# Two more empty steps between the scaling of the context's rows and their transposes

## The chip, the cores and the metric

The kernel runs on one core of a Trainium2 chip. The metric is the time on the device in microseconds (us) of one execution, the median of several runs. The core has TensorE (PE in the profile; PEld is its loading of stationary operands), VectorE (DVE), ScalarE (ACT), GpSimd (POOL) and SyncE (SP), which here only issues DMAs. Each engine works through its own instruction queue; semaphores make one wait for another.

## The reference, cut to what matters

One layer of a diffusion backbone over 2048 latent tokens of width 1024, with a prefix of 256 context tokens. The change touches the part in which the context's keys and values are made:

```python
mod_c = jax.nn.silu(c_ctx) @ w_mod[l] + b_mod[l]
sh1c, sc1c, ... = jnp.split(mod_c, N_MOD, axis=-1)
h_c = modulate(ctx_s, norm1_g[l], sh1c, sc1c)      # rmsnorm(ctx) * g * (1 + scale) + shift
p_c = h_c @ w_in[l][:, :KV_COLS]                   # 256 x 1024 times 1024 x 256
k_c = rmsnorm(kv_heads(p_c[..., :K_W]), k_norm_g[l])
v_c = kv_heads(p_c[..., K_W:KV_COLS])
h_x = modulate(x, norm1_g[l], sh1, sc1)
p_x = h_x @ w_in[l]                                # 2048 x 1024 times 1024 x 3840
...
```

The latent tokens' projection `p_x` yields keys, values, queries, the two inputs of the spatial gating, and two gate logits. Attention over all latent and context keys, the gating, a merge, an output projection and an MLP follow.

## The kernel before

**Precision and products.** Every float32 product is done with operands split into a high and a low part, by a cast on ScalarE (or VectorE) and a subtraction on VectorE, and as three products on TensorE (`product`, lines 1744, 1745 and 1746: high by high, high by low, low by high). Large products use seven block products in place of eight, in the order `SUMS = (0, 1, 5, 6, 4, 2, 3)`; the sums of weight blocks that this needs are called terms. They are made on VectorE, written to `t_d` in memory, and loaded again (line 710) when their block product is due. The line 712 casts such a load and line 713 forms its low part.

**The projection** (`project`) runs over two blocks of 1024 tokens. In each, `pairs_run` goes through two pairs of weight column blocks: first pair 0 (keys, values, queries; 384 columns a block), then pair 1 (gating inputs; 512 columns). A pair is 14 steps: seven block products, two halves of the inner dimension each. A step is four token tiles of six products. In the first token block the run is split: pair 0, then the gates of two weight groups (`gates`, groups 0 and 1), then pair 1, then the other six groups.

**Work beside it.** Three kinds of side work are threaded into these steps as Python generators:

- `opening` (line 1136) is continued at two points of each pair step, by `next(opens, None)` in `along` (line 1197). In pair 0 that makes 28 visits, in pair 1 more; during the gates it is not continued. It first finishes the second token block's operands; then it lets visits pass until `CONTEXT_AT = 20` and hands over to `context_keys` (line 1176).
- `self.work` is a list of generators, of which `tick` (line 762) continues the first by one piece: twice a pair step, once a gate step. It holds the keys' work (`keys_work`, line 799: norm, rotation, split, transposes, store), the queries' work (`queries_work`, line 837), the weight terms of pair 1 (`terms`, line 664), the preparation of the spatial weights (`gm_consts`) and so on, in the order in which they were put in. The weight terms are put in at place 1 when pair 0 is done.
- the gate weights' preparation, advanced by the gate steps.

**`context_keys`** (line 963) loads the context's two row tiles (line 966), waits one visit, computes the root mean square and scales the rows (`h_scale`: squares on ScalarE, line 515; the reciprocal root on VectorE, lines 163 to 179, in which several other sums also run; the scaling on ScalarE, line 528), waits one visit, takes a bank for the accumulator `acc`, and then goes in four visits over the inner dimension, two rows of 128 at a time: a load of 256 KB of weights (line 976) and its split (lines 153 to 157), four transposes (line 999), the modulation on ScalarE (line 1003), a split, and the 12 products of the visit before. The products of the fourth part come at the visit after it, with the copies of keys and values out of `acc` (lines 1011 and 1014), the store of the values (line 1015), and this line, which puts the rest of the context's work behind what the list holds by then:

```python
        self.work += [self.keys_work(nt, None, kraw), self.gm_consts()]
```

**Tiles.** On-chip memory is divided into rings of slots by tag. Those that matter are "m" (four slots of 4 KB a partition) and "t2" (six), and the banks of TensorE's accumulators, four "a" for the pairs' tiles and four "b" for everything else (transposes, context, and the gate groups 0 and 1). In the profile the tags show as m, t, a and b. The context's row tiles, its split operands w and h, the squares, the queries' tiles and the weight terms' tiles are all of tag "m".

**Order.** The program's order of emission is the priority of an instruction. A scheduler fills each engine's queue at build time, taking the first by priority of those that its own model holds ready, so work of a lower priority can be put ahead of work that isn't ready. `order` (line 2069) adds that tiles of one tag are handed out in emission order; pinned stretches keep the engines' order as written, but the work of the change lies in none of them.

Of the kernel before, what the change touches and what calls it, by code (L numbers as in the profile page):

```python
# [72 lines left out]
class Kern:  # L73
# [889 lines left out]
    def context_keys(self):  # L963
        nc = self.nc
        nt = CTX // P
        xs = self.x_load(self.I["ctx"][0], nt, self.m4)
        yield
        self.h_scale(xs)
        yield
        acc = self.bank([nt, CTX])  # L970
        staged = None
        for k0 in range(0, KC + 2, 2):
            done, staged = staged, None
            if k0 < KC:
                raw = self.t2([2, 256])
                nc.sync.dma_start(
                    raw,
                    self.I["w_in"][0][k0 * P : (k0 + 2) * P, :256].rearrange(
                        "(k p) c -> p k c", p=P
                    ),  # L980
                )
            if done:
                w, h = done
                for j in range(2):
                    for t in range(nt):
                        tok = slice(t * P, (t + 1) * P)
                        a = (h[:, 0, j, tok], h[:, 1, j, tok])
                        self.product(
                            acc[:, t], [a], [(w[:, 0, j], w[:, 1, j])],
                            k0 == 2 and j == 0 and t == 0,  # L990
                        )
            if k0 < KC:
                w, h = (self.m4([2, 2, CTX], F32R) for _ in range(2))
                self.split(raw, w[:, 0], w[:, 1], lo_eng="dve")
                ps = self.bank([2, CTX])
                tmp = self.t2([2, CTX])
                for j in range(2):
                    for t in range(nt):
                        nc.tensor.transpose(
                            ps[:, j, t * P : (t + 1) * P], self.columns(xs[t], k0 + j),  # L1000
                            self.ident,
                        )
                    nc.scalar.activation(
                        tmp[:, j], ps[:, j], AF.Identity,
                        scale=self.G1[:, k0 + j, 1:2], bias=self.S1[:, k0 + j, 1:2],
                    )
                self.split(tmp, h[:, 0], h[:, 1], hi_eng="dve", lo_eng="dve")
                staged = (w, h)
                yield
        kraw, V = self.t2([TT, NKV, HD]), self.t2([TT, NKV * HD])  # L1010
        nc.vector.tensor_copy(
            kraw[:, :nt].rearrange("p t h d -> p t (h d)"), acc[:, :, :P]
        )
        nc.scalar.copy(V[:, :nt, :], acc[:, :, P:])
        nc.scalar.dma_start(self.vc_d[:, :nt], V[:, :nt])
        self.work += [self.keys_work(nt, None, kraw), self.gm_consts()]
        yield
# [1417 lines left out]
```

## Time and profile before

| | us |
|---|---|
| median of 3 runs | 3008.2 (3007.79 to 3643.23) |
| profiled execution, its own time | 3012.09 |
| its span | 3010.1 |
| mean granted TensorE clock | 0.993 |

The profile is of one execution. A row of its time-ordered view has the start and the duration in us, the engine, the line of the kernel, the operation, output and inputs by tag, and the shape; in brackets stand the idle time of that engine just before and what ended it. The chain of waits lists what ended last at each moment, with start and duration. A row of the table by stretches has the busy time and the instruction count of each engine, the granted TensorE clock (1.00 is full), the DMA engines' busy share and GB/s. Matmuls overlap, so their durations add up to more than the time they take.

The page's slices of 1/40 of the span (75.25 us each), busy tenths of TensorE and VectorE:

```profile
PE   7899999999999999999999989999999999999999
...
DVE  5857487766888887867555587776676766654555
```

The projection's first token block fills the first slices; the context's rows are loaded at 88.52 us, and the transposes of line 999 run from 110.75 to 126.8 us:

```profile
88.52 1.53 SPq L505 DMA_DIRECT2D m<-in_ctx  x2
...
104.37 0.46 SPq L976 DMA_DIRECT2D t<-in_w_in  x1
...
124.78 0.42 SPq L976 DMA_DIRECT2D t<-in_w_in  x1
```

The four weight loads of line 976 are issued by SyncE between 104.37 and 124.78 us.

### The profile page before, as it was taken

The page shows a single profiled execution, that of the slowest core. Times are in us where ns is not written, and L with a number is a line of the kernel's source. Part 1 is how long each engine was busy: PE and PEld are TensorE (multiplying, and loading weights), DVE is VectorE, ACT ScalarE, POOL GpSimd, SP SyncE. Part 2 cuts the span into 40 slices and gives each one's busy share as a digit, 9 for nine tenths or more (in the row PEclk, how much of TensorE's full clock was granted, in tenths as well). Part 3 has the DMA queues.
Part 4 walks back from the last instruction along what each step waited for, and adds up shares of the span by engine and source line. Part 5 has one row for each costly group of instructions (what it writes and reads, how often), then busy time and mean ns, then how long its engine had stood idle before and what let it go on. Part 6 is the DMA issues. An engine that isn't in the chain of part 4 may idle for free.

```text
span 3010.1 us, 37936 instructions
## 1 busy us (share of the span) xinstructions
PE 2931.4 (97%) x13325; PEld 2210.1 (73%) x13325; DVE 2069.9 (69%) x2983; ACT 1418.8 (47%) x2318; POOL 650.8 (22%) x470
## 2 busy tenths in 40 slices
PE   7899999999999999999999989999999999999999
PEld 5778788876455555556888878888887888888887
DVE  5857487766888887867555587776676766654555
ACT  5544865554454544444222354444454344444432
POOL 0000000001899898894212200000000000000000
PEclk9999999999999999999999999999999999999999
DMA  7687967774010010016776658888766544447554
GB/s 274 186 293 262 315 205 225 253 245 150 24 36 29 22 37 22 22 35 189 238 215 194 183 198 308 310 301 304 263 216 223 185 154 154 154 158 272 210 208 156
DMA packets 386175, 559.04 MB, mean 186 GB/s; under 512 B 38640, under 2 KB 192416, under 8 KB 385984
## 3 DMA queue, kind: packets, MB, share of 16 engines
q1 hardware_dynamic: 373616, 535.89, 53.7%
q10 hardware_dynamic: 12368, 20.73, 1.9%
q8 instruction: 105, 1.72, 0.2%
q14 instruction: 86, 0.70, 0.1%
HBM read 379.75 MB, written 176.69 MB: 185 GB/s over the span
## 4 chain that ended last, share of the span: by engine, by line
PE 82%; DMA 6%; DVE 6%; ACT 3%; issue 2%; SPq 1%; ACTq 0%; POOL 0%; DVEq 0%; POOLq 0%
PE b L1744 14%; PE b L1745 14%; PE b L1746 14%; PE b L2322 8%; PE b L2291 4%; PE b L2310 4%; PE b L186 4%; PE b L187 4%; PE b L188 4%; PE b L2246 3%; PE a L1744 2%; PE a L1746 2%; PE a L1745 2%; PE b L192 1%; DMA m<-ws_d 1%
## 5 line engine op out<-in xcount | busy, mean ns | idle before, releaser
L2257 DVE TENSOR_REDUCE ts<-b 128x1 f32<-128x512 f32 x492 | 302.0, 681 | 69.7 <-PE b L2246 69.7
L2342 POOL TENSOR_TENSOR ac<-ac,p 128x512 f32<-128x512 f32 x214 | 306.1, 1463 | 54.5 <-ACT p L2314 54.5
L1860 DVE TENSOR_TENSOR b<-b,b 128x1024 fp32r<-128x1024 f32 x170 | 200.7, 1221 | 137.1 <-ACT b L1859 136.3
L1859 ACT CAST b<-b 128x1024 fp32r<-128x1024 f32 x170 | 170.6, 1051 | 225.3 <-PE b L1746 100.1
L2314 ACT ACTIVATE p<-b 128x512 f32<-128x512 f32 x384 | 194.0, 624 | 175.5 <-PE b L2310 168.3
L1745 PE MATMUL b<-b,b 128*128 128x512 f32 x680 | 265.2, 390 | 3.6 <-DVE b L1860 3.5
L1744 PE MATMUL b<-b,b 128*128 128x512 f32 x680 | 266.2, 391 | 1.7 <-DVE f L1881 1.5
L1746 PE MATMUL b<-b,b 128*128 128x512 f32 x680 | 264.7, 389 | 0.0
L2342 POOL TENSOR_TENSOR ac<-p,p 128x512 f32<-128x512 f32 x32 | 51.5, 1629 | 746.1 <-DMA raw<-in_w_mod 736.8
L2342 POOL TENSOR_TENSOR ac<-ac,t 128x512 f32<-128x512 f32 x152 | 204.1, 1374 | 0.0
L2291 PE MATMUL b<-h,h 128*128 128x512 f32 x576 | 187.3, 405 | 3.3 <-ACT p L2314 2.2
L2322 PE MATMUL b<-p,h 128*64 128x512 f32 x768 | 187.3, 611 | 0.0
L2310 PE MATMUL b<-h,h 128*128 128x512 f32 x576 | 178.6, 391 | 0.0
L1745 PE MATMUL b<-hb,b 128*128 128x512 f32 x446 | 173.8, 390 | 0.0
L1754 DVE TENSOR_TENSOR f<-f,b 128x512 f32<-128x512 f32 x160 | 109.2, 682 | 78.4 <-issue 45.7
L1744 PE MATMUL b<-hb,b 128*128 128x512 f32 x415 | 161.9, 390 | 0.0
L1746 PE MATMUL b<-hb,b 128*128 128x512 f32 x415 | 161.3, 389 | 0.0
L1745 PEld LDWEIGHTS b<-b,b 128*128 128x128 f32 x680 | 127.6, 188 | 32.2 <-DVE b L1860 5.5
L2291 PEld LDWEIGHTS b<-h,h 128*128 128x128 f32 x576 | 103.6, 188 | 63.8 <-DVE ts L2257 24.3
L1744 PEld LDWEIGHTS b<-b,b 128*128 128x128 f32 x680 | 127.6, 188 | 29.9 <-ACT b L1859 2.8
L1746 PEld LDWEIGHTS b<-b,b 128*128 128x128 f32 x680 | 127.7, 188 | 26.5
L157 POOL TENSOR_TENSOR bw<-bw,bw 128x512 fp32r<-128x512 f32 x58 | 75.9, 1331 | 235.6 <-ACT bw L153 233.8
(440 smaller groups left out, 7243.0 us busy)
## 6 DMA issues: line engine op xcount, KB each, us to landing
ao_d<-f SPq DMA_DIRECT2D x224, 256.0 KB
f<-in_w_ff SPq DMA_DIRECT2D x48, 1024.0 KB
b<-ao_d SPq DMA_DIRECT2D x85, 512.0 KB
b<-w2o_d SPq DMA_DIRECT2D x85, 512.0 KB
w2o_d<-f SPq DMA_DIRECT2D x112, 256.0 KB
f<-in_w_in SPq DMA_DIRECT2D x38, 512.0 KB
f<-x_d SPq DMA_DIRECT2D x64, 256.0 KB
hb<-ao_d SPq DMA_DIRECT2D x54, 256.0 KB
```

The source lines that it names most:

```text
L186: mm(ps, sh, mh, start=start, stop=False)
L1744: mm(ps, wh, hh, start=start and k == 0, stop=False, skip_group_check=True)
L1745: mm(ps, wh, hl, start=False, stop=False, skip_group_check=True)
L1746: mm(ps, wl, hh, start=False, stop=k == len(w) - 1, skip_group_check=True)
L1859: nc.scalar.copy(h, f32(l))
L1860: nc.vector.tensor_tensor(out=l, in0=f32(l), in1=f32(h), op=ALU.subtract)
L2257: nc.vector.tensor_reduce(out=self.mx[:, t, h, c : c + 1], in_=ps[h], axis=AX.X, op=ALU.max)
L2291: self.nc.tensor.matmul(self.pts[j][h], k.KA[c][self.kv][:, ks], self.qa[h], start=True, stop=False, skip_group_check=True,)
L2310: self.nc.tensor.matmul(s, k.KB[c][self.kv][:, ks], self.qb[h], start=False, stop=True, skip_group_check=True,)
L2314: self.nc.scalar.activation(pt[h], s, AF.Exp)
L2322: nc.tensor.matmul(self.o[h * HD : (h + 1) * HD, :], k.V[c][:, i, self.kv * HD : (self.kv + 1) * HD], pt[h], start=j == 0, stop=j == NKT - 1,)
L2342: nc.gpsimd.tensor_tensor(out=self.acc[e][:, h], in0=old[:, h], in1=pt[h], op=ALU.add)
```

## The change

In `context_keys`, the one empty visit between `h_scale` and the accumulator's bank becomes three:

```diff
         xs = self.x_load(self.I["ctx"][0], nt, self.m4)
         yield
         self.h_scale(xs)
-        yield
+        for _ in range(3):
+            yield
         acc = self.bank([nt, CTX])
         staged = None
         for k0 in range(0, KC + 2, 2):
```

No instruction is added or removed. Counted from 0, the visits of `opening` in pair 0 were used like this: 20 loads the rows, 21 scales them, 22 to 25 take the four parts, 26 the last products and copies, 27 nothing. With the change 20 and 21 stay, 22 and 23 are empty, 24 to 27 take the four parts, and the last products, the copies and the line that extends the work list come at the first visit in pair 1, after the eight gate steps between the pairs.

## The prediction

> **What bounds the kernel now.** I read the page first (busy time by engine), then the table by stretches of time for the projection's first token block, then the chain of work that ended last inside the stretch that sticks out, and then the time-ordered rows of the tiles that the change moves.
>
> ```profile
> span 3010.1 us, 37936 instructions
> ...
> PE 2931.4 (97%) x13325; PEld 2210.1 (73%) x13325; DVE 2069.9 (69%) x2983; ACT 1418.8 (47%) x2318; POOL 650.8 (22%) x470
> ```
>
> TensorE is busy for 97% of the span. The change adds no arithmetic, so all it can win is TensorE's idle time, 3010.1 - 2931.4 = 78.7 us in the whole kernel, plus what a lowered clock costs after a pause. What it can lose is a new pause.
>
> The stretches, 20 us each (columns: busy time and count of each engine, granted clock, DMA share, GB/s):
>
> ```profile
> core 0: us, PE busy (x) PEld busy (x) DVE busy (x) ACT busy (x) POOL busy (x), PEclk, DMA share, GB/s
> 100.00:120.00 20.00, 12.29 (x58) 10.99 (x57) 15.14 (x47) 9.25 (x15) 0.00 (x0) 0.74 0.56 175
> 120.00:140.00 20.00, 20.00 (x121) 17.19 (x120) 15.41 (x25) 13.83 (x23) 0.00 (x0) 1.00 0.66 198
> 160.00:180.00 20.00, 18.73 (x82) 14.85 (x81) 10.05 (x14) 6.50 (x10) 0.00 (x0) 1.00 0.97 348
> 180.00:200.00 20.00, 17.73 (x76) 14.37 (x75) 11.03 (x27) 7.83 (x14) 0.00 (x0) 0.94 0.86 276
> ```
>
> 100 to 120 us is where the context's rows are scaled and first transposed: TensorE works 12.29 of 20 us there, at a mean granted clock of 0.74. From 120 us on it is full. At 160 to 200 us it loses 1.27 and 2.27 us while the DMA engines are 97% and 86% busy; that stretch matters for the risk below. GpSimd does nothing in any of them.
>
> The transposes that the change moves (line 999), in order of time, with the idle time ahead of them in brackets:
>
> ```profile
> 110.75 0.47 PE L999 MATMUL b<-ident,m 128*128 128x128 f32 x1 [5.34 <-ACT m L528]
> 111.79 0.47 PE L999 MATMUL b<-ident,m 128*128 128x128 f32 x1 [0.57 <-ACT m L528]
> 112.98 0.69 PE L999 MATMUL b<-ident,m 128*128 128x128 f32 x2 [0.71 <-ACT t L1003]
> ...
> 114.76 0.69 PE L1744 MATMUL a<-f,hx 128*128 128x384 f32 x1 [1.09 <-ACT a L734]
> ```
>
> TensorE stood from 105.41 to 110.75 us for the first scaled row tile, then 0.57, 0.71 and 1.09 us more: 7.71 us in all. The chain of waits says why the scaling was late (start, duration, what):
>
> ```profile
> 100.03 6.28 DMA f<-t_d
> ...
> 106.39 0.84 ACT f L712
> ...
> 107.25 0.96 DVE f L713
> 108.21 0.08 DVE ts L179
> ...
> 109.30 0.17 DVE ts L179
> ...
> 109.55 2.19 ACT m L528 x2
> 111.74 0.72 ACT f L712
> ...
> 114.32 0.39 ACT a L734
> ```
>
> A weight load of the first pair (f<-t_d) took 6.28 us. ScalarE's cast of it (line 712) and VectorE's subtraction (line 713) stand in their engines' queues ahead of the last steps of the reciprocal root (line 179), so the root ended at 109.47, the two scalings at 111.74. The context's arithmetic was ready earlier; it stood behind somebody else's DMA.
>
> **The change part by part.** (1) Two more empty visits. They issue no instruction: count and bytes stay. What moves is emission order, which is the priority by which the scheduler fills each engine's queue. The generator is visited twice per step of the first pair, and a step is 24 products of 384 columns, which the chain shows at 0.17 us apiece once the clock is back:
>
> ```profile
> 115.45 0.32 PE a L1745
> ...
> 120.53 0.22 PE b L999 x2
> ...
> 121.27 0.17 PE a L1746
> ```
>
> So the transposes (16), their ScalarE passes (8), the splits, the four 256 KB loads of the key/value weights on SyncE's queue and the 48 products all come 24 x 0.17 = 4.1 us of TensorE work later. GpSimd's queue holds none of them; the store of the context's values on ScalarE's queue moves with them. The loads of the rows and the scaling stay where they are.
>
> (2) What happens at 105.41. With the transposes behind it, TensorE's next work is the first pair's next step, line 1744. It needs the weights that landed at 106.31 (high part 107.23, low part 108.21, by the chain) and the accumulator that VectorE's line 2127 and ScalarE's line 734 give back:
>
> ```profile
> L2127 DVE TENSOR_TENSOR t<-t,a x4: 545/546/548, 110.0 to 117.0; 128x384 f32<-128x384 f32 x4
> ```
>
> The first of these four started at 110.0, behind line 713, the root and one split of the context's weights. The split moves away; line 713 does not. Soonest, line 2127 follows line 713 directly: 108.21 + 0.55 + 0.45 for the copy (0.39 in the chain, plus hand-over) = about 109.3 (an estimate). Latest, the copy stands behind both scalings and the second cast, 111.74 + 0.72 + 0.45 = 112.9. I take 111.0, between them, since one of four tiles can go early and the other three queue behind the scalings. Against 114.76 that wins 3.7 us. Off go the four transposes that filled part of the gap; they now run in the stream, at 0.22 us for two by the chain's row: -0.5. Net gain 3.2 us, bounds 1.4 (from 112.9) and 5.0 (from 109.3).
>
> The clock has a row of its own: products take 0.32 us at 115.45 and 0.17 at 121.27, so the 4.2 us of work up to about 119 lost some 2 us. I count no gain there, since even the soonest resume leaves 3.9 us of pause. The Trainium skill, "TensorE: Matmul & The Clock Gate", section "HAM oscillation — how this bites in real kernels", says that a pause over about 3.4 us drops TensorE to half clock, and a shorter one need not. The trace agrees in the size (5.34 us of pause, then 0.32 against 0.17). By that rule a pause cut under 3.4 us would win the 2 us as well, and the sum would end 2 us lower.
>
> (3) Where the end of the context falls. Before, the four transposing visits and the final one fit the 28 visits of the first pair with one to spare (20th loads, 21st scales, 22nd to 25th, final products and copies at the 26th). Two later, the last products, the copies out of the accumulator, and the queueing of the context's key work and of the spatial weights' preparation come at the first visit in the second pair, behind the eight gate steps that run between. Two things are then held longer: one of four "b" banks, and two of the four "m" slots (the last split operands w and h), which are handed out in emission order.
>
> ```profile
> 127.01 0.37 SPq L842 DMA_DIRECT2D m<-p_d  x1
> ...
> 133.87 2.01 ACT L779 ACTIVATE m<-m 128x1024 f32<-128x1024 f32 x2 [1.42 <-PE b L1746]
> ...
> 146.57 0.68 DVE L491 TENSOR_TENSOR m<-m,t 128x512 f32<-128x512 f32 x1
> ...
> 168.28 0.59 ACT L2184 COPY t<-b 128x512 f32<-128x512 f32 x1 [2.06 <-PE b L1746]
> ...
> 196.15 0.52 PE L192 MATMUL b<-ident,m 128*128 128x128 f32 x3 [2.27 <-DVE m L821]
> ...
> 198.22 1.23 DVE L713 TENSOR_TENSOR f<-f,f 128x1024 fp32r<-128x1024 f32 x1 [2.22 <-ACT f L712]
> ...
> 207.94 0.58 ACT L729 COPY t<-a 128x512 f32<-128x512 f32 x1
> ```
>
> Already now the queries' work waits for these slots: their squares (133.87) started when the last context product ended. With the change the queries' two tiles hold two slots and the last context operands the other two, and the rotation (line 491, 146.57) can't get a tile until the final products have run. They are ready at about 138 (133.9 + 4.1) by data, but in priority they stand behind gate products that end at 168.28. TensorE takes them in any moment in which the gates' products are not ready; there are several hand-overs of accumulators through ScalarE in that time, and 12 products of 256 columns need under 2 us. I take it that they get through before 146.57, and cost this at 0; what covers it is named in the rivals, with its price.
>
> (4) The context's key work goes behind the second half's keys and queries. The 2.27 us pause at 196.15 was for its transposes, placed right behind the second pair's weight terms; another key work (line 799 too, with rotation) now stands in that place, so I leave the pause as it is: 0, bounds -2.3 and +2.
>
> Sum: 3.2 won, 0 and 0, rounded to 3. The profiled execution took 3012.09 us (span 3010.1 and 2.0 around it); less 3 is 3009. It stands 3.9 us above the median of the runs, 3008.2, so against that median I predict 3005.
>
> **The rivals.** Handed on: the pause only changes its name. For it speaks that the late DMA, and the two engines' queues behind it, stay, and that line 734 was itself late; against it, that 1.6 us of the gap is refilled by the moved transposes and that VectorE's split goes away. Gain 1.4 or less, and a random microsecond or two from the new order: 3007 to 3010.
>
> Whole pause gone: the scheduler also pulls line 2127 ahead of line 713, so TensorE hardly stops. 7.7 us and 2 us of clock, less 0.5: 9.2 won, 2999. Against it, the weights' low part is not there before 108.21.
>
> Slower, by slots: the final context products do wait for the gates. Then the rotation starts at about 168.3, 21.7 us after 146.57, and with it the second pair's weight terms, which need all four "m" slots for each quarter. The last of them that TensorE wants early is ready at 198.22 + 1.23 = 199.45; the accumulator that takes its products first is read at 207.94, so they begin a good microsecond before that and there are some 7 us of slack (an estimate). Past that TensorE, which has nothing else of the pair to do, waits: 21.7 - 7 = 14.7, less the 3.2 won: 3020; with the clock lowered by such a pause and the DMA engines 97% busy in that stretch, up to 3024. It decides from final products later than about 146.6 + 7 = 153.6. For it: emission order, the full 20.00 us of TensorE at 120 to 140. Against it: the products are short and ready long before.
>
> That the change doesn't do what it says (the scheduler issues the same order as before, since the transposes wait for the same tiles) would give 3008; I count it with the handed-on case.
>
> **How the numbers follow.** Forecast (about 3 us won, 3002 to 3007) 0.45; handed on, or same order 0.22; slower by slots 0.23; whole pause gone 0.10. The likeliest gives 3005. The range takes in the whole pause gone (2999) and the slots' case to 3024: 2998 to 3024, with about 0.15 left out for effects on the order further on. 2% of this kernel is 60 us, about what its measurement can tell from no change, and no case reaches it: a gain of 60 us would need three quarters of TensorE's 78.7 us of idle time. Faster by over 2% 0.01, within 2% 0.95, slower by over 2% 0.04, the last for a pause of the slots' kind that repeats.
>
> **What would show it.** Right: the 5.34 us ahead of line 999 gone, its place taken by 4 to 6 us ahead of line 1744, which names line 734; the 100 to 120 us stretch above 12.29 us busy by 2 to 4; the final context products (256 columns, lines 1744 to 1746) before 147, the rotation's first row at about 146. Wrong: those products after 154 and pauses of TensorE at 195 to 215 that name line 713 or a load of t_d (slots); a busy time of 16 or more at 100 to 120 (whole pause gone). If a difference over 10 us comes from behind 330 us, where neither operand is alive any more, the reasoning misses a cause.

## The result, and the profile after

| | before | after |
|---|---|---|
| median of 14 runs, us | 3005.92 | 3014.90 |
| lowest | 2999.75 | 3011.74 |
| profiled execution, own time | 3012.09 | 3016.92 |
| its span | 3010.1 | 3015.1 |

The ratio of the changed kernel to the one before is 1.0031, with a 95% interval of 1.0021 to 1.0041: some 9 us slower, where 3 us faster was forecast. One run of before, of 3643.23 us, is slow and stands outside that ratio. The time lies in the stated range (2998 to 3024), on the wrong side.

TensorE's busy time did not grow (2929.6 us by the page of after, 2931.4 before), so the longer span of the profiled execution is idle time (85.5 us against 78.7). The table by stretches of the changed kernel (columns as before: busy time and count of PE, PEld, DVE, ACT, POOL, then granted clock, DMA share, GB/s):

```profile
100.00:120.00 20.00, 16.58 (x80) 15.25 (x79) 15.33 (x48) 10.33 (x18) 0.00 (x0) 0.83 0.65 206
...
180.00:200.00 20.00, 16.32 (x72) 13.14 (x71) 6.40 (x9) 3.89 (x6) 0.00 (x0) 0.98 0.91 304
200.00:220.00 20.00, 4.83 (x15) 3.88 (x16) 13.02 (x30) 9.67 (x16) 0.00 (x0) 0.50 0.83 282
```

At 100 to 120 us TensorE works 16.58 us in place of 12.29: 4.3 us won. At 200 to 220 us it works 4.83 us, at half clock, where before it worked all 20:

```profile
200.00:220.00 20.00, 20.00 (x95) 16.36 (x95) 12.96 (x31) 12.01 (x20) 0.00 (x0) 0.98 0.92 312
```

The time-ordered rows of TensorE in the changed kernel name what ended those pauses (in brackets, idle time before the row and who ended it; from line 970 on its lines are one higher than before, so 1745 is before's 1744):

```profile
109.23 0.45 PE L1745 MATMUL a<-f,hx 128*128 128x384 f32 x1 [2.55 <-ACT a L734]
109.84 0.45 PE L1746 MATMUL a<-f,hx 128*128 128x384 f32 x1 [0.16 <-DVE f L713]
111.95 1.07 PE L1745 MATMUL a<-f,hx 128*128 128x384 f32 x2 [0.71 <-ACT f L712]
...
212.44 1.94 PE L192 MATMUL b<-ident,m 128*128 128x128 f32 x8 [16.13 <-DVE m L821]
217.11 0.79 PE L1745 MATMUL a<-f,h 128*128 128x512 f32 x1 [2.73 <-ACT a L727]
```

The 7.71 us of pauses around the context's first transposes became 3.42 us, on the first pair's own work. What remained is the late weight load and its cast, on ScalarE ahead of the copy (line 734) that gives the accumulator back:

```profile
107.96 0.83 ACT L712 CAST f<-f 128x768 fp32r<-128x768 f32 x1 [5.68 <-DMA f<-t_d]
108.70 0.48 ACT L734 COPY a<-t 128x384 f32<-128x384 f32 x1
...
114.69 2.19 ACT L528 ACTIVATE m<-m,ts 128x1024 f32<-128x1024 f32 x2 [0.19 <-DVE ts L179]
```

VectorE's part of giving it back (before's line 2127) ran ahead of its subtraction for those weights (line 713):

```profile
106.53 0.55 DVE L2128 TENSOR_TENSOR t<-t,a 128x384 f32<-128x384 f32 x1
108.83 0.96 DVE L713 TENSOR_TENSOR f<-f,f 128x768 fp32r<-128x768 f32 x1 [1.75 <-ACT f L712]
```

In exchange there are 16.13 + 2.73 = 18.86 us at 196 to 217 us, where before had one pause of 2.27 us. Line 192's transposes at 212.44 belong to the key work of the second half of the token block. Why they were late is read backwards, in VectorE's rows of the changed kernel:

```profile
163.14 0.69 DVE L491 TENSOR_TENSOR m<-m,t 128x512 f32<-128x512 f32 x1 [5.57 <-PE b L1747]
...
172.31 0.69 DVE L679 TENSOR_TENSOR m<-m 128x512 f32<-128x512 f32 x1 [0.27 <-DMA m<-in_w_in]
...
203.82 0.68 DVE L682 TENSOR_TENSOR m<-m,m 128x512 f32<-128x512 f32 x1
204.60 0.69 DVE L780 TENSOR_REDUCE ts<-m 128x8 f32<-128x512 f32 x1
...
211.62 0.68 DVE L821 TENSOR_TENSOR m<-t,m 128x512 fp32r<-128x512 f32 x1
```

The queries' rotation (line 491) began at 163.14, not at 146.57, and its releaser is TensorE's line 1747, a product. The weight terms of pair 1 (lines 679 to 682) follow it and ended at 203.82 + 0.68 = 204.5. The key work's squares waited for line 681 of that last quarter and started at 203.94, so its sums and its last step, line 821, came only then. The product that released the rotation is the last of the context's, in TensorE's rows:

```profile
150.68 0.28 PE L1747 MATMUL b<-m,m 128*128 128x256 f32 x1
150.79 0.28 PE L1745 MATMUL b<-m,m 128*128 128x256 f32 x1
...
151.03 0.28 PE L1747 MATMUL b<-m,m 128*128 128x256 f32 x1
162.24 0.28 PE L1745 MATMUL b<-m,m 128*128 128x256 f32 x1
...
162.83 0.28 PE L1747 MATMUL b<-m,m 128*128 128x256 f32 x1
```

The last twelve context products (256 columns) came in two halves: six from 149.75 to 151.03, and six from 162.24, with eleven microseconds of gate products between. Before, the last one ran at 133.55.

Why even the first half came so late is seen in ScalarE's rows. Before, the cast of the fourth part's weights (line 153) came ahead of the queries' squares (line 779, at 133.87):

```profile
130.39 0.62 ACT L153 CAST m<-t 128x512 fp32r<-128x512 f32 x1 [2.39 <-PE b L1746]
```

In the changed kernel the squares come first. They wait for the products of the third part, and the cast of the fourth part follows them:

```profile
144.09 2.01 ACT L779 ACTIVATE m<-m 128x1024 f32<-128x1024 f32 x2 [2.17 <-PE b L1747]
...
146.47 0.62 ACT L153 CAST m<-t 128x512 fp32r<-128x512 f32 x1
```

VectorE's last split of that part ended at 150.46 us. From then on all twelve products were ready by data, and six of them still stood until 162.24.

ScalarE's rows show that the late key work also blocked what was ready. Its queue has the squares (line 779) and the copies of the transposes (line 833) ahead of the copies that hand pair 1's accumulators on (lines 2126 and 727):

```profile
203.94 0.63 ACT L779 ACTIVATE m<-t 128x512 f32<-128x512 f32 x1 [8.02 <-DVE m L681]
...
213.57 0.58 ACT L833 COPY t<-b 128x512 f32<-128x512 f32 x1 [1.41 <-PE b L192]
...
215.47 1.08 ACT L2126 COPY t<-a 128x512 f32<-128x512 f32 x2
```

By the first product of the attention's preparation, the changed kernel is 15.9 us behind (it starts at 696.2 us before, 712.1 after). The pauses account for 18.86 - 2.27 - 4.29 = 12.3 us of this; the rest isn't taken apart here. The attention itself then took 638.3 us before and 629.5 after (first to last product of its scores: 735.1 to 1373.4, 750.1 to 1379.6), which gives 8.8 us back in these two executions; the last section comes back to that.

### The profile page after: what moved, and what is told of

Read it like the earlier page. It is cut to its first block, busy times and chain, and to the rows that moved or that the text cites. A ratio compares the mean times of both kernels' runs of the same rounds, so it can differ in the third digit from the quotient of the medians.

```text
span 3015.1 us, 37951 instructions
## 1 busy us (share of the span) xinstructions
PE 2929.6 (97%) x13325; PEld 2212.7 (73%) x13325; DVE 2066.0 (69%) x2983; ACT 1418.4 (47%) x2318; POOL 653.7 (22%) x470
## 4 chain that ended last, share of the span: by engine, by line
PE 85%; DVE 6%; DMA 5%; ACT 2%; issue 2%; SPq 0%; POOL 0%; DVEq 0%; ACTq 0%; POOLq 0%
PE b L1745 14%; PE b L1747 14%; PE b L1746 14%; PE b L2323 9%; PE b L2292 4%; PE b L2311 4%; PE b L186 4%; PE b L187 4%; PE b L188 4%; PE b L2247 3%; PE a L1745 2%; PE a L1746 2%; PE a L1747 2%; PE b L192 1%; DMA m<-ws_d 1%
## 5 line engine op out<-in xcount | busy, mean ns | idle before, releaser
L1745 PE MATMUL a<-f,h 128*128 128x384 f32 (+1 forms) x320 | 119.6, 378 | 12.8 <-ACT h L572 4.4
```

The source lines that it names most:

```text
L1745: mm(ps, wh, hh, start=start and k == 0, stop=False, skip_group_check=True)
```

## The experiments

Three theories. S, slots: the last context operands hold two of the four "m" slots, so the queries' rotation and behind it the weight terms are late. L, list: the second half's key work, longer by its rotation, stands in the place where the context's stood. D, distance: every visit of delay costs its share. Ratios are to runs of the kernel before on the same chip, taken beside each kernel; its median there lay between 3005.9 and 3011.1 us, so medians of different rows can't be compared. The pauses are TensorE's, from its time-ordered rows at 190 to 222 us.

| kernel | last context product, us | rotation starts, us | pauses, us | ratio, 95% interval |
|---|---|---|---|---|
| before | 133.55 | 146.57 | 2.27 | 1 |
| after | 162.83 | 163.14 | 16.13, 2.73 | 1.0031 (1.0021 to 1.0041) |
| e1_one | 136.52 | 146.59 | 1.16, 1.92, 2.15 | 0.9975 (0.9965 to 0.9984) |
| e2_flush | 148.88 | 153.34 | 4.52, 4.30 | 1.0010 (0.9997 to 1.0023) |
| e3_split | 149.72 | 152.95 | 9.95, 2.73 | 1.0006 (0.9996 to 1.0017) |
| e7_all_late | 165.56 | 165.88 | 16.53, 2.73 | 1.0034 (1.0022 to 1.0047) |
| e4_idle8 | 160.32 | 160.64 | 9.49 | 1.0113 (1.0099 to 1.0127) |
| e5_scale_early | 129.64 | 143.14 | 1.25, 2.26 | 0.9979 (0.9968 to 0.9989) |
| e6_all_early | 135.46 | 152.20 | 1.70 | 1.0014 (1.0004 to 1.0025) |
| e8_t4 | 144.91 | 145.84 | 1.24, 1.73, 2.23 | 0.9985 (0.9975 to 0.9995) |

**One empty visit more in place of two.**

```diff
-        for _ in range(3):
+        for _ in range(2):
             yield
```

> One more empty visit instead of two, so that the context's last products still fall into the first pair's 28th visit, ahead of the gates. Theory S (slots: what costs is that the last context operands hold two of the four m slots over the eight gate steps): the rotation of the queries starts by 150 us, no pause over 4 us at 190 to 215, part of the 105 us pause is won: 3002 to 3006 beside 3006 for before. Theory D (distance: each visit of delay costs its share): half of the loss, 3010. Theory L (list: the second half's key work stands ahead of the context's): list order is as before, so no loss either, 3002 to 3006.

Faster than before: the pause ahead of the first transposes is gone, the last products still fall into the first pair, and the rotation starts where it did before. D falls: half of the delay costs nothing. Where the gain of the ratio arises the profile does not show: that execution took 3009.32 us, the slowest of its ten, and its attention's preparation starts at 702.7 us against 696.2.

**The last products before the gates.** In the first of two kernels, the visit of the fourth part also does the last products, the copies and the extension of the work list; in the second only the last products.

```diff
                 staged = (w, h)
-                yield
+                if k0 + 2 < KC:
+                    yield
```

> Two more empty visits, but the last products, the copies and the extension of the work list come in the same visit as the fourth part, ahead of the gates. S: the rotation starts at about 151 (the operands' part of the lateness stays, the wait behind the gates goes), the pause at 212 falls from 16 to 4 to 8 us: 3004 to 3009. L: list order as before, pause as before (2 to 3 us), 3002 to 3005. D: as the changed kernel, 3013 to 3016.

The second has this besides:

```diff
+        yield
         kraw, V = self.t2([TT, NKV, HD]), self.t2([TT, NKV * HD])
```

> As e2_flush, but the copies and the extension of the work list stay behind the gates; only the last products come ahead of them. S: as e2_flush, 3004 to 3009, with the second half's key work in the place of the pause. L: as the changed kernel, a pause of 13 to 17 us at 205 to 215 and 3013 to 3016.

In both, the rotation starts at 153 us: 10 us of its lateness were the wait behind the gates, and some 6.5 us remain. Those are the order of the ring. In the changed emission the queries' tiles come ahead of the context's second to fourth operands, and their squares ahead of the fourth, so these wait for slots, also when their products do not wait for the gates. The pauses allow a rough division: 8.82 us in e2_flush and 12.68 in e3_split, which differ in the list order and in the place of the copies, so L is worth some 3.9 us; the wait behind the gates the next 6.2 (12.68 to 18.86); the ring's order the first 6.6 (2.27 to 8.82). Each is from one profile, and the pause of before was 2.27 us in one execution and 0.58 in another (r_before below), so they are no better than 1 to 2 us. Neither theory had the 12.68 us of e3_split: S expected 4 to 8, L 13 to 17. TensorE's rows of e3_split (its line numbers are three higher than before's, those of e2_flush two), with the second half's key work in the place of the pause, as S had it:

```profile
204.48 1.94 PE L192 MATMUL b<-ident,m 128*128 128x128 f32 x8 [9.95 <-DVE m L821]
209.15 0.79 PE L1747 MATMUL a<-f,h 128*128 128x512 f32 x1 [2.73 <-ACT a L727]
```

The same rows of e2_flush, where the context's key work stands there again and the spatial weights' load behind it:

```profile
204.50 0.98 PE L192 MATMUL b<-ident,m 128*128 128x128 f32 x4 [4.52 <-DVE m L821]
209.78 0.47 PE L192 MATMUL b<-ident,t 128*128 128x128 f32 x1 [4.30 <-DMA t<-in_gm_ws]
```

The ratios of these two do not tell them apart.

**The whole context two visits later, with the distance of before.**

```diff
-CONTEXT_AT = 20
+CONTEXT_AT = 22
...
-        for _ in range(3):
+        for _ in range(1):
             yield
```

> One empty visit as before, but the loads and the scaling start two visits later too (22 in place of 20). S and L: the same crossing of the gates, rotation after 160 us and a pause of 13 to 17 us at 205 to 215; at 105 us nothing of the context is due, so up to as much is won there as in the changed kernel: 3012 to 3018. If the distance between the scaling and the transposes were what wins at 105 us, line 1000 would again have a pause of over 4 us ahead of it: 3017 to 3021.

The same loss as the changed kernel, by the same two pauses. At 105 us TensorE waited 2.47 us for line 734, as after; the transposes had pauses of 0.71 and 1.07 us of their own. Eleven of the last twelve products had run by 154.26 us; the last one, of 0.28 us, ran at 165.56, and the rotation followed it. So the place behind the gates costs, and not the distance between scaling and transposes.

**The key work later.** The changed kernel with eight idle pieces in the work list behind the weight terms.

```diff
                         self.work.insert(1, self.first_terms)
+                        self.work.insert(2, self.idle(8))
...
+    def idle(self, n):
+        for _ in range(n):
+            yield
```

> The changed kernel with eight idle pieces put into the work list behind the weight terms, so that the second half's key work is emitted eight pieces later. Theory L (the pause is the key work's squares and transposes, placed at the head of ScalarE's and TensorE's queues, holding back ready products): the 16.1 us pause falls under 6, 3003 to 3007. Theory S (the weight terms themselves are late by the slots): the first half of the block product of the terms runs, then TensorE waits 6 to 12 us for a load of t_d or line 713: 3008 to 3013.

```profile
209.17 1.22 PE L1750 MATMUL a<-f,h 128*128 128x512 f32 x2 [9.49 <-ACT f L712]
```

With the key work out of the way, TensorE runs the products that were ready, then waits 9.49 us for the cast (line 712) of a load of terms (line 1750 is before's 1744). So the late terms alone cost 9.5 us here, as S had it, and the key work at the head of the queues added some 9.4 us of the 18.86. The rotation was 14.07 us later than before (160.64 against 146.57), so the terms had some 4.6 us of slack (an estimate, if their lateness is the rotation's). As a whole this kernel is far slower, 1.0113, which neither theory had: with every later piece of side work pushed back by eight, TensorE loses time at 680 to 720 us (11.38 and 7.10 us busy in two stretches of 20, before 20.00 and 19.61), and it starts the attention's preparation at 728.9 in place of 696.2. So its ratio says nothing on S or L; only the pause does.

**Loads and scaling two visits earlier, the rest in its old place.**

```diff
-CONTEXT_AT = 20
+CONTEXT_AT = 18
```

> Three empty visits, but loads and scaling two visits earlier (18 and 19), so that the four parts and the last products keep the places of before (22 to 26). S and L: no crossing, no pause over 4 us at 190 to 215, and the pause ahead of line 1000 goes below 4 us: 2998 to 3004, faster than before. If the late scaling is due to the DMA at 100 us alone, the pause ahead of the transposes stays at 5 us: 3004 to 3008.

Faster than before, as is e1_one; the two intervals overlap, so neither is the better by these runs. The pauses at 104 to 109 us are 0.66 and 2.24 us, and the late pauses stay small. In its profile this lead is gone by the attention's preparation, which starts at 696.8 us, so here too the source of the ratio's gain isn't shown.

**The whole context two visits earlier.** CONTEXT_AT is 18 with one empty visit.

> One empty visit as before, the whole context two visits earlier (18 in place of 20). S: no crossing, no loss at 190 to 215; the distance between scaling and transposes is as before, so a pause ahead of line 1000 stays unless the weight load that delays the scaling isn't in its way there: 3000 to 3008. Tells whether the place or the distance made the pause at 105 us.

A miss for S: slower than before. The early transposes meet the same late weight loads, and now the splits and modulations wait too, with VectorE at work from 107.97 to 123.21 us almost without a gap: six pauses between 105 and 126 us of 1.21, 2.08, 1.11, 3.24, 4.08 and 0.93 us, 12.65 together against 7.71. The rotation starts at 152.2 without any pause over 1.7 us later, since TensorE was late itself: what seems to count is the rotation's lateness against TensorE's own progress.

**Other slots for the context's operands.** The changed kernel, with nothing moved.

```diff
-                w, h = (self.m4([2, 2, CTX], F32R) for _ in range(2))
+                w, h = (self.t4([2, 2, CTX], F32R) for _ in range(2))
```

> The changed kernel, with the context's split operands taken from the ring t4 (eight slots) in place of m (four); every product stays where the change put it. S: the queries' tiles no longer wait for the last context operands, the rotation starts by 150 us, the pause at 212 falls under 6: 3002 to 3007 (unless the gates now wait for t4). L: the list order is unchanged, pause 13 to 17 us, 3012 to 3016.

The loss is gone (0.9985 against 1.0031), though the list order is that of the changed kernel and the last products still come behind the gates in emission. The rotation is back at 145.84, ahead of the value of before. The queries' first load, which waited for a slot until 127.48 us in the changed kernel, is issued at 105.67:

```profile
105.67 0.39 SPq L842 DMA_DIRECT2D m<-p_d  x1
116.16 0.37 SPq L843 DMA_DIRECT2D m<-p_d  x1
```

The last twelve products, still emitted behind the gates, were ready at 138.92 us, by the end of VectorE's last split, and ran in two groups among the gate products, the first and the last of them being:

```profile
140.80 0.28 PE L1745 MATMUL b<-t,t 128*128 128x256 f32 x1
...
144.91 0.28 PE L1747 MATMUL b<-t,t 128*128 128x256 f32 x1
```

This settles the cause: the four slots of tag "m". It also shows that the place behind the gates in emission costs little while the operands come in time and the queries don't wait for their slots.

**The attention's start.** In the kernel before, the first of VectorE's sums in the first attention unit was put on GpSimd.

```diff
-        e = j in (LAST_ON_VECTOR if self.last else ON_VECTOR)
+        first = (self.b, self.p) == (0, 0) and j == 4
+        e = j in (LAST_ON_VECTOR if self.last else ON_VECTOR) and not first
```

> The kernel before, with the first of VectorE's sums in the attention's first unit (key tile 4) put on GpSimd. In the profile of before that VectorE addition took 6.75 us against 1.79 in the changed kernel's, and TensorE paused 3.54 us behind it at a lowered clock; the attention took 638 against 630 us. If that instruction, held up by GpSimd's row of additions, is what makes the attention longer in before: no VectorE addition over 4 us at 755 to 770, attention 628 to 632 us, ratio 0.997 to 0.999. If the hold-up only moves to the next sum: ratio 0.999 to 1.001.

No gain: 1.0009 (0.9999 to 1.0018). The hold-up moved to the next sum, which took 5.61 us, as the second case had it. Together with e5_scale_early:

> e5_scale_early (loads and scaling two visits earlier, three empty visits) and the sum of c2_gather together. If both savings are real and lie apart in time: ratio 0.994 to 0.997, the best so far. If e5_scale_early's advantage was itself the luck of the attention's start: 0.997 to 0.999.

0.9983 (0.9974 to 0.9992), no better than e5_scale_early alone. This number was expected for the case of luck, but as c2_gather saved nothing that could be added, it does not tell whether e5_scale_early's gain was luck. Then one more profiled execution of each of the two kernels:

> The changed kernel once more, for a second profile. Theory S gives the same pauses in it at 107 and 212 us, within 1 us, since they come from queue orders. If the short VectorE addition at the attention's start (1.79 us) belongs to the kernel, it comes again; if it is chance of one execution, it may take over 5 us here.

> The kernel before once more, for a second profile. The pauses at 110 us (5.3 us) and 196 us (2.3 us) come again within 1 us. If the long VectorE addition at the attention's start (6.75 us) belongs to the kernel, it comes again; if it is chance of one execution, it may take under 2 us here, and the attention 630 us.

The pauses of the changed kernel came again (3.53 us at 108 us, 15.28 and 2.73 at 210 to 215). In the kernel before those ahead of the transposes did (6.88, 0.56, 0.71 and 1.08 us), but the first was 1.5 us longer and the one at 196 us, of 0.58, was 1.7 us shorter, so neither was within 1 us as expected. The pauses at the transposes' place thus fell from 9.23 to 3.53 us in this pair of profiles, and from 7.71 to 3.42 in the other. The attention's preparation starts at 694.3 us before and 713.8 after, the spans are 3005.6 and 3022.7. The VectorE addition took 6.77 us before and 6.74 after. In the changed kernel it had taken 1.79 us in the first profile, so its length belongs to the execution; for the kernel before both profiles have the long form.

## Why the prediction was wrong

**The bound and the pause at 105 us: right in kind, its size in part by luck.** TensorE's idle time was what could be won or lost. TensorE resumed behind line 734, as forecast, and the pauses there fell by 4.3 us (5.7 in the second pair of profiles), against 3.2 with bounds of 1.4 to 5.0. But the path was another. The forecast put VectorE's line 2127 behind line 713, soonest at 109.3 (its terms add up to 109.21), most likely at 111.0. It ran at 106.53, ahead of line 713, and what was left was ScalarE's cast ahead of line 734. TensorE also stopped later, at 106.68 in place of 105.41, so that 2.55 us stood ahead of the first product where the prediction looked for 4 to 6. And the scaling, said to stay where it was, started at 114.69 in place of 109.55. That the clock was given no gain came true, but not for the reason given: at 114.73 us the products of the changed kernel still take 0.32 us each, though the pause was shorter than the 3.9 us on which the prediction relied.

**The fall of the context's end: this step failed.** It said of the last products "I take it that they get through before 146.57, and cost this at 0". They ended at 163.1. Two things were wrong in it. The operands of the fourth part were not ready at about 138 us, as a shift by 4.1 us would have it, but at 150.46: the ring hands its slots out in emission order, and two visits of delay put the queries' tiles ahead of the context's second to fourth operands and their squares ahead of the fourth. I had named the slots, and shifted the old times instead of walking the new order. And six of the twelve short products then stood for eleven microseconds behind gate products of higher priority; "any moment in which the gates' products are not ready" did not come for them in that time. With other slots (e8_t4) the operands were ready at 138.92 and the products through by 145.2, as the step had it. So it was the slots that broke it.

**The key work's place: this step failed too.** It said that another key work stands in the same place, "so I leave the pause as it is: 0, bounds -2.3 and +2". The pause became 18.86 us. It was wrong to cost it alone: standing at the head of three queues is cheap while its input is in time, and this input was behind the weight terms that the step before had made late. The list order by itself was worth some 3.9 us by e2_flush and e3_split, outside its bounds as well.

**The slots' rival was what happened.** I gave it 0.23. It put the rotation at 168.3 and the wait at 14.7 us; it started at 163.14 and the pauses are 18.86 us, since the slack of seven microseconds was some 4.6 (e4_idle8), and the key work ahead of the ready products took more than that away. So its sign came only in part: the products ran after 154, but the pauses name lines 821 and 727, the key work, and not line 713 or a load of t_d. Its time of 3020 lies above the median of 3014.9. Part of that difference may be the attention's start, which differs from one execution to the next; this isn't shown.

## What to carry to other kernels

When emission order also hands out the slots of a small ring, a step that moves later moves behind every other user of the ring that is emitted in between: write down the new order of requests, tile by tile, before shifting any old time. A short piece of work that frees a scarce slot should be emitted ahead of long work of the same engine, since a busy engine may have no gap to fit it in (eleven microseconds here). To undo a pause caused by a late input, moving the input's producer earlier (e5_scale_early) or the consumer by less (e1_one) won, by the ratios, where moving the consumer past a stage boundary lost.

## What the runs showed of the hardware

One VectorE addition of two operands in on-chip memory, 128x1024, took 1.2 us as a rule, but 6.75 us at the attention's start in the kernel before. VectorE's row of that kernel:

```profile
758.38 6.75 DVE L2339 TENSOR_TENSOR ac<-p,t 128x1024 f32<-128x1024 f32 x1
```

GpSimd's rows at that place, the last with the idle time ahead of it:

```profile
759.06 4.99 POOL L2342 TENSOR_TENSOR ac<-ac,p 128x512 f32<-128x512 f32 x4
765.96 2.51 POOL L2342 TENSOR_TENSOR ac<-ac,p 128x512 f32<-128x512 f32 x2 [1.91 <-ACT p L2314]
```

It ended 1.1 us after a row of four GpSimd additions had ended (764.05), so it seems to have stood through all four. The Trainium skill, "SBUF — State Buffer", section "Who interferes with whom", says that a VectorE instruction with two inputs in SBUF contends with a GpSimd instruction that reads SBUF, for a pair of ports which is an exclusive lock. The trace fits that, but here the wait lasted for four instructions of about 1.25 us and not for one. In the profiled execution of the changed kernel it took 1.79 us:

```profile
773.26 1.79 DVE L2340 TENSOR_TENSOR ac<-p,t 128x1024 f32<-128x1024 f32 x1
```

Both began some 0.7 us ahead of the start of a GpSimd row, at 759.06 and 773.91. In the changed kernel that row's six additions took 1.41 us each on average:

```profile
773.91 8.47 POOL L2343 TENSOR_TENSOR ac<-ac,p 128x512 f32<-128x512 f32 x6
```

So it seems that VectorE got in ahead of that row there, and only behind it in the kernel before. What decides this is not shown.

In the profile of before TensorE paused 3.54 us behind the long form. Over the attention's first 40 us the granted clock was 0.91 to 0.96 in seven of the eight profiles with the long form named below, and 1.00 in e5_scale_early and in the four without it. The attention took 629.4 to 629.5 us in the four profiles with the short form (after, e1_one, e3_split, e7_all_late) and 632.0 to 638.3 in the eight with the long one, c2_gather and c3_early_gather aside. Both forms occur in executions of one and the same program, the changed kernel. How often each comes, whether a kernel's timing favours one, and how far that shifts a median stays open; between single executions the attention's difference of 2.5 to 8.9 us is up to as large as the change's effect.

The second surprise is the clock. In the changed kernel a pause of 2.55 us, ended at 109.23, and one of 0.16 were enough to lower it. It fell between 110 and 111 us, ahead of the pause of 0.71 us, as the table by stretches of 1 us shows (the third value from the right is the granted clock):

```profile
109.00:110.00 1.00, 0.60 (x2) 0.35 (x3) 1.00 (x3) 0.18 (x1) 0.00 (x0) 1.00 0.24 89
110.00:111.00 1.00, 1.00 (x5) 0.73 (x5) 1.00 (x5) 0.45 (x1) 0.00 (x0) 0.78 0.01 3
111.00:112.00 1.00, 0.29 (x2) 0.05 (x1) 1.00 (x4) 1.00 (x3) 0.00 (x0) 0.50 0.13 46
```

The chain of waits shows how long it stayed low (start, duration, what):

```profile
114.73 0.32 PE a L1746
...
116.97 0.32 PE a L1747
...
117.74 0.17 PE a L1747
```

The Trainium skill, "TensorE: Matmul & The Clock Gate", section "HAM oscillation — how this bites in real kernels", puts the limit at pauses of over about 3.4 us. The measurement differs: the prediction weighed that a cut below that limit might win 2 us of clock; the pause was cut below it, and the clock fell all the same.
